# Encoder trunk: low parts, channel sums, first taps, reciprocals and sigmoids change engine or place

## The chip, the cores and the metric

The kernel runs on one core of a Trainium2 chip. The metric is the device time of one execution in microseconds (us). TensorE (PE) does the matmuls and the transposes, VectorE (DVE) and GpSimd (POOL) the elementwise work, ScalarE (ACT) the activations and scaled copies. Each engine works through its own queue in order, and waits there for semaphores of the others.

## The reference

Two sequences (256 and 512 tokens, 768 in all) go through two layers of the same shape; the width is 1024.

```python
def conv_module(u, w_dw, b_dw, ln_g, ln_b, w_pw):
    a, g = jnp.split(u, 2, axis=-1)
    z = a * jax.nn.sigmoid(g)
    z = lax.conv_general_dilated(z, w_dw[:, None, :], ...) + b_dw   # 31 taps, per channel
    z = jax.nn.silu(layer_norm(z, ln_g, ln_b))
    return z @ w_pw

for l in range(DEPTH):                       # 2 layers
    h = rms_norm(x, g_mix[l])
    q, k, v, u, gl = jnp.split(h @ w_in[l], splits, axis=-1)
    ...                                      # rms norm and rotary positions of q and k
    a = blocked_attention(q, k, v)           # 8 heads of 128, 2 heads of k and v
    c = conv_module(u, ...)
    ga, gc = jnp.split(jax.nn.sigmoid(gl + b_gate[l]), 2, axis=-1)
    x = x + (ga * a + gc * c) @ w_out[l]
    gate, up = jnp.split(rms_norm(x, g_ffn[l]) @ w_gu[l], 2, axis=-1)
    x = x + (jax.nn.silu(gate) * up) @ w_down[l]
return rms_norm(x, g_final)
```

## The kernel before

Matmuls are done in three passes over split operands: each float32 factor is a high part (rounded by ScalarE, names `hi_`) and a low part (the difference, names `lo_`), and hi·hi, lo·hi and hi·lo are summed. Of the weights ScalarE makes the high parts and GpSimd the low parts, in units of 128x1024 (two column tiles, `size == 2`) or in quarters; `wu` are the weights of the convolution's input u, `wqkv` those of q, k and v, `wgl` of the gates, `wpw` of the pointwise convolution, `wo` of the output projection, `wd` of the down projection.

A layer has these stretches. First come the projections for the convolution's input, k and q, then attention in 48 steps: a step is a head h and a tile t of 128 queries, named `h3t0` and so on. A step's scores (`h3t0s`) are three matmuls; VectorE takes the row maximum (TENSOR_REDUCE into `st`), ScalarE the exponential and its row sum, VectorE the reciprocal, ScalarE scales the probabilities (`h3t0p`), and TensorE transposes them (`h3t0T`) one step later. Between scores and transposes TensorE's queue has "fill": projections of v, q, u (`ug`, `ua`) and the gates (`gl`), later the pointwise convolution (`c`). After attention follow the output projection and the feed-forward part, the longest stretch.

The depthwise convolution is VectorE's. The 1024 channels are 8 tiles of 128; each tile's gated input is a padded buffer `z` (there are three, `N_Z = 3`), and its output `y` of 128x783 comes from 31 taps: the first is `y = z*w0 + b`, the others are `y = z*wk + y`. Sums of the eight `y` over the tiles go to `ysum`, the squares to `sq`. From them the channel norm is made: two matmuls with ones give `mean`, 8 centrings (`y - mean`, VectorE), 8 squares (ScalarE) and 7 adds (VectorE), six small matmuls `var`, an inverse root on GpSimd (`vs`), its spread `rb`, six transposes `rstd`, 8 scalings (VectorE), then silu and the split into `zsh` and `zsl`, which the pointwise convolution `c` multiplies.

The order is written out by the host program. `Clock` models TensorE's time as matmuls are issued (`now`) and VectorE's (`dve`, by 1/960 us per element and 0.13 per operation). Whenever the model shows VectorE less than 1.0 us ahead, it issues the next tap, from one of two tiles in turn; what is due at a time waits in a heap. Two places break this pace. A new `z` (in `ag_half`) is only begun when at most two are live, and until then all outstanding taps of the oldest are issued in one burst; GpSimd then zeroes the borders of the new `z` (the MEMSETs), which waits until the last tap on the old one is done. And before the first matmul of `c`, `pw_body` calls `force`, which issues, without any TensorE work between them, all taps and all parts of the channel norm that are still outstanding.

Of the kernel before, what the change touches and what calls it, by code (L numbers as in the profile page):

```python
# [13 lines left out]
F32 = mybir.dt.float32  # L14
F32R = mybir.dt.float32r
BF16 = mybir.dt.bfloat16
AF = mybir.ActivationFunctionType
ALU = mybir.AluOpType
AX = mybir.AxisListType

P = 128
D = 1024
KC = D // P
# [21 lines left out]
CONV_N = ZP - 2 * PAD  # L45

V_GMIX, V_GFFN, V_GFIN, V_BDW, V_LNG, V_LNB, V_BGATE, V_WDW = 0, 8, 16, 24, 32, 40, 48, 64
# [6 lines left out]
class Clock:  # L54
# [21 lines left out]
    def tick(self):  # L76
        while self.heap and self.heap[0][0] <= self.now:
            heapq.heappop(self.heap)[2]()
        while self.dve < self.now + TAP_AHEAD and self.tap():
            pass  # L80
# [38 lines left out]
class Vector:  # L119
# [5 lines left out]
    def __getattr__(self, name):  # L125
        f = getattr(self.engine, name)

        def call(out, *args, **kw):
            n = 1
            for d in (args[0].shape if name == "tensor_reduce" else out.shape)[1:]:  # L130
                n *= d
            self.clock.vector(n / 960.0 + 0.13)
            return f(out, *args, **kw)  # L133
        return call

# [20 lines left out]
def trunk(tc, x_in, x_tok, w_a, w_qkv, w_pw, w_out, w_gu, w_down, vecs, gqk, rope, y_out):  # L156
    nc = tc.nc
    clock = Clock()
    vector = Vector(nc.vector, clock)

    with ExitStack() as ctx:
        cst = ctx.enter_context(tc.tile_pool(name="cst", bufs=1))
# [35 lines left out]
        def vcol(l, base, j):  # L198
            return vec[:, l * VEC + base + j: l * VEC + base + j + 1]
# [88 lines left out]
        class Weights:  # L288
# [48 lines left out]
            def pump(self):  # L337
                while self.load():
                    pass
                if self.ready < len(self.all) and clock.now >= self.next:  # L340
                    w = self.all[self.ready]
                    if self.here(w) and self.live + w.size + max(self.staged, N_WS) <= N_W:
                        self.split()

            def get(self, w):
                while w.out is None:
                    self.split()
                return w.out

            def free(self, w):  # L350
# [278 lines left out]
        def layer_blocks(l):  # L629
            y = Layer()  # L630
# [126 lines left out]
            def conv(j, z):  # L757
                wcol = lambda k: vcol(l, V_WDW, k * KC + j)

                def first():  # L760
                    y.y[j] = UC(nm(f"y{j}"))
                    vector.tensor_scalar(y.y[j], z[:, :CONV_N], wcol(0), vcol(l, V_BDW, j), op0=ALU.mult, op1=ALU.add)

                def tap(k):
                    def f():
                        vector.scalar_tensor_tensor(y.y[j], z[:, k:k + CONV_N], wcol(k), y.y[j],
                                                    op0=ALU.mult, op1=ALU.add)
                    return f

                def last():  # L770
                    y.z_live -= 1
                    tap(CK - 1)()
                    clock.at(1.5, add)

                def add():
                    if y.ysum is None:
                        y.ysum = XP(nm("ysum"))[:, :CONV_N]
                        nc.gpsimd.tensor_copy(y.ysum, y.y[j])
                    else:
                        engine = vector if y.convs == KC - 1 else nc.gpsimd  # L780
                        engine.tensor_tensor(y.ysum, y.ysum, y.y[j], op=ALU.add)
                    y.convs += 1
                    if y.convs == KC:
                        clock.at(LN_AFTER, lambda: channel_norm(y))

                taps = [tap(k) for k in range(1, CK - 1)] + [last]
                clock.waiting.append([first] + taps)

            def ag_half(j, ws, w0, s, part):
                if s == 0:  # L790
# [63 lines left out]
            for b in FILL:  # L854
                kind, _, n = b.partition(":")
                n = int(n or 0)
# [258 lines left out]
            def down7(c0):  # L1115
# [40 lines left out]
                def then(b):  # L1156

                    after = list(BURSTS[b]) if b < len(BURSTS) else []
                    if tail and b == 3:
# [6 lines left out]
                def part(b):  # L1166
                    ms = BURSTS[b]

# [122 lines left out]
        def attention(y):  # L1291
            l, nm = y.l, y.nm
# [6 lines left out]
            def scores(n):  # L1299
                h, t, s, un = unit(n)  # L1300
                stream.until((l, f"q:{h // 2}"))
                for f in y.k_flip:
                    f()
                qs, fs = y.q[h // 2]
                fs[h % 2]()
                (qhi, qlo), (khi, klo) = qs[h % 2], y.k[h // GROUP]
                k0, nk = SPLITS[s]
                tk = slice(t * P, (t + 1) * P)
                sc = PS(un + "s")
                for p, (qq, kk) in enumerate(((qhi, khi), (qlo, khi), (qhi, klo))):  # L1310
                    mm(sc[:, :nk], qq[:, tk], kk[:, k0:k0 + nk], p == 0, p == 2)
                r = y.srq[h // 2][:, 2 * t + h % 2:2 * t + h % 2 + 1]
                sm = S(un + "st", 4)
                clock.tick()
                vector.tensor_reduce(sm[:, 0:1], sc[:, :nk], axis=AX.X, op=ALU.max, negate=True)
                p32 = HT(un + "p")
                probs[n] = p32

                def exp():
                    act(sm[:, 1:2], sm[:, 0:1], AF.Copy, scale=r)  # L1320
                    act(p32[:, :nk], sc[:, :nk], AF.Exp, scale=r, bias=sm[:, 1:2], accum_out=sm[:, 2:3])

                late = stream.done((l, FILL[-1]))
                jobs[n] = [
                    clock.later(A_EXP, exp),
                    clock.later(A_REC[late], lambda: vector.reciprocal(sm[:, 3:4], sm[:, 2:3])),
                    clock.later(A_SCALE[late], lambda: act(p32[:, :nk], p32[:, :nk], AF.Copy, scale=sm[:, 3:4])),
                ]

            def flip(n):  # L1330
                h, t, s, un = unit(n)
                nkt = SPLITS[s][1] // P
                if t % 2 == 0:
                    pairs[n // 2] = (XP(un + "pThi", (P, 4, 256), F32R), XP(un + "pTlo", (P, 4, 256), F32R))
                hi, lo = pairs[n // 2]
                p32 = probs.pop(n)
                for job in jobs.pop(n):
                    job()
                tp = PS(un + "T")
                for c in range(nkt):  # L1340
                    turn(tp[:, c * P:(c + 1) * P], p32[:, c * P:(c + 1) * P])
                t3 = tp[:, :nkt * P].rearrange("p (c q) -> p c q", q=P)
                dst = (slice(None), slice(0, nkt), slice((t % 2) * P, (t % 2 + 1) * P))
                clock.tick()
                act(hi[dst], t3)
                jobs.setdefault(("lo", n // 2), []).append(
                    clock.later(PT_LO, lambda: sub_lo(vector, lo[dst], t3, hi[dst])))
# [32 lines left out]
            def fill():  # L1380
                goal[0] += FILL_US / 2
                if not stream.done((l, FILL[-1])):
                    stream.run(goal[0], (l, FILL[-1]))
                    if stream.done((l, FILL[-1])):
                        goal[0] = stream.work
                        goal[0] += PW_START
                        y.late = clock.now + 8.0
                        y.h_free = 2
                        split_z(y)
                elif y.m_done:  # L1390
                    goal[0] = max(goal[0] + (LATE_US - FILL_US) / 2, stream.work)
                    stream.run(goal[0], (l, f"pw:{min(y.m_done, PW_MAX) - 1}"))

            NU = H * NT
            for n in range(NU + VLAG):
                if n < NU:
                    scores(n)
                if n >= VLAG and (n - VLAG) % 2 == 0:
                    values((n - VLAG) // 2)
                if n < NU and n % NT == 3 and n // NT % 2 == 0:  # L1400
                    y.q[n // NT // 2][1][1]()
                fill()
                if 1 <= n <= NU:
                    flip(n - 1)
                if clock.now >= y.late:
                    flush(y)
                fill()
            for f in outs:
                f()

# [3 lines left out]
        def channel_norm(y):  # L1414
# [59 lines left out]
            def scale(j):  # L1474
                def f():
                    for s, (t0, n) in enumerate(SPLITS):
                        sl = slice(YO[s], YO[s] + n)
                        vector.tensor_tensor(ys[j][:, sl], ys[j][:, sl], rstd[s][:, :n], op=ALU.mult)
                    if j in SILU_AT:
                        clock.at(0.5, lambda: silus(j))  # L1480
# [53 lines left out]
        nc.gpsimd.memset(ones, 1.0 / D)  # L1534
        nhalf = cst.tile([P, 16], F32, name="nhalf")
        nc.gpsimd.memset(nhalf, -0.5)


        y = layers[0]
# [69 lines left out]
        "gl:10", "gl:2", "q:2", "ag:7", "gl:3", "gl:14", "gl:12", "gl:4", "gl:11", "q:3", "gl:5", "gl:13", "gl:7",  # L1609
        "gl:15", "gl:6"]  # L1610
SILU_AT = (5, 7)
BURSTS = ((1, 7), (6, 4), (5, 2), (3,))
D_FIRST = (4.0, 6.0)
D_AT = 0.5
# [23 lines left out]
RSTD_AFTER = 5.4  # L1638
TABLES_AT = 16.0
TAP_AHEAD = 1.0  # L1640
W_STEP = (0.9, 2.9)
A_EXP = 2.2
A_REC = (4.5, 2.5)
A_SCALE = (4.9, 4.0)
PT_LO = 1.4
M_AT = 2.5
# [88 lines left out]
```

## Time and profile before

| | us |
|---|---|
| median of 3 runs (2399.19 to 2402.68) | 2401.75 |
| the profiled execution's own time | 2401.79 |
| its span, first to last instruction | 2400.0 |
| busy: TensorE, VectorE | 2235.7, 1933.2 |
| busy: ScalarE, GpSimd | 1134.3, 1285.0 |

The span lacks 1.8 us of the execution's own time, which lie before its first and after its last instruction. TensorE's granted clock is 0.972 of full speed over the whole span. Both layers show the same stretches at a distance of some 1187.5 us. Rows of a timeline join equal instructions that follow each other on an engine (x3); a bracket at the end gives the idle time before a row and who ended it.

### The profile page before, as it was taken

Reading aid. Unit: us, or ns where it says so; the run is one execution under the profiler, and the core shown is the slowest. Engines: PE = TensorE matmul, PEld = TensorE weight load, DVE = VectorE, ACT = ScalarE, POOL = GpSimd, SP = SyncE. Lnnn points to the kernel's source line nnn. Section 1 sums busy time; section 2 is a strip of 40 time slices with the busy share of each in tenths; the row PEclk is TensorE's granted clock in tenths of the full one; section 3 lists DMA queues with packets and bytes.
Section 4 is the critical chain, followed back from the end, with each engine's and each line's share of the span. In section 5 each row is a group of like instructions: output and inputs, shape, how many; then the busy total and the mean of one; then the engine's idle time right before and its main releaser. Section 6 shows DMA issues by size and latency. Waiting matters only on the chain. (4 is left out here: it accounts for less than half of the span.)

```text
span 2400.0 us, 34938 instructions
## 1 busy us (share of the span) xinstructions
PE 2235.7 (93%) x13276; PEld 2101.9 (88%) x13276; DVE 1933.2 (81%) x2480; ACT 1134.3 (47%) x2281; POOL 1285.0 (54%) x956
## 2 busy tenths in 40 slices
PE   8888898999979999999998899999999799999997
PEld 7878787888979999999987788878889799999997
DVE  5899999855387798798978999997553887887888
ACT  5425564684244444444443255647843444444443
POOL 4933554442266666666668344535323766756664
PEclk9999999999989999999999899999999899999999
DMA  4111111133313343343421111112341133334332
GB/s 168 36 62 62 52 58 60 64 101 137 113 44 110 119 141 123 124 141 110 156 82 53 53 47 57 58 62 78 111 170 53 44 121 135 129 118 141 123 123 88
DMA packets 72425, 229.60 MB, mean 96 GB/s; under 512 B 8128, under 2 KB 15296, under 8 KB 72256
## 3 DMA queue, kind: packets, MB, share of 16 engines
q1 hardware_dynamic: 72256, 227.37, 27.7%
q8 instruction: 104, 1.70, 0.3%
q14 instruction: 65, 0.53, 0.1%
HBM read 208.46 MB, written 18.87 MB: 95 GB/s over the span
## 5 line engine op out<-in xcount | busy, mean ns | idle before, releaser
L133 DVE SCALAR_TENSOR_TENSOR L_y<-L_z,vec,L_y 128x783 f32<-128x783 f32 x480 | 638.7, 1363 | 2.5
L214 POOL TENSOR_TENSOR wq_L_wgu_0m<-T_L_wgu,wq_L_wgu_0m 128x512 fp32r<-128x512 f32 x168 | 228.5, 1375 | 172.5 <-ACT wq_L_wgu_0m L211 172.5
L211 ACT ACTIVATE wq_L_wgu_0m<-T_L_wgu 128x512 fp32r<-128x512 f32 x168 | 102.7, 630 | 257.6 <-DVE T_L_wgu L133 204.4
L214 POOL TENSOR_TENSOR wq_L_wgu_0m<-st_L_wgu,wq_L_wgu_0m 128x512 fp32r<-128x512 f32 x126 | 179.3, 1424 | 43.3 <-ACT wq_L_wgu_0m L211 42.6
L203 PE MATMUL L_gl<-L_h1h,hi_L_wgl 128*128 128x512 f32 (+1 forms) x512 | 181.5, 355 | 0.3 <-DVE L_q3r L133 0.2
L203 PE MATMUL L_gl<-L_h1h,lo_L_wgl 128*128 128x512 f32 (+1 forms) x512 | 176.1, 344 | 0.0
L203 PE MATMUL L_gl<-L_h1l,hi_L_wgl 128*128 128x512 f32 (+1 forms) x512 | 176.0, 344 | 0.0
L214 POOL TENSOR_TENSOR lo_L_wgl<-st_L_wgl,hi_L_wgl 128x1024 fp32r<-128x1024 f32 x32 | 87.8, 2745 | 147.1 <-ACT hi_L_wgl L211 116.5
L214 POOL TENSOR_TENSOR lo_L_wqkv<-st_L_wqkv,hi_L_wqkv 128x1024 fp32r<-128x1024 f32 x24 | 69.0, 2877 | 137.1 <-ACT hi_L_wqkv L211 132.1
L214 POOL TENSOR_TENSOR lo_L_wu<-st_L_wu,hi_L_wu 128x1024 fp32r<-128x1024 f32 (+1 forms) x32 | 85.9, 2685 | 61.4 <-ACT hi_L_wu L211 61.4
L203 PEld LDWEIGHTS L_gl<-L_h1h,lo_L_wgl 128*128 128x128 f32 x512 | 99.0, 193 | 11.6
L203 PEld LDWEIGHTS L_gl<-L_h1h,hi_L_wgl 128*128 128x128 f32 x512 | 99.3, 194 | 10.7 <-DVE L_q3r L133 0.7
L203 PEld LDWEIGHTS L_gl<-L_h1l,hi_L_wgl 128*128 128x128 f32 x512 | 99.2, 194 | 10.3 <-issue 0.5
L214 POOL TENSOR_TENSOR lo_L_wo<-st_L_wo,hi_L_wo 128x1024 fp32r<-128x1024 f32 x16 | 39.6, 2476 | 116.0 <-ACT hi_L_wo L211 116.0
L203 PE MATMUL L_ua<-L_h1h,lo_L_wu 128*128 128x256 f32 (+1 forms) x256 | 89.0, 348 | 6.2 <-POOL lo_L_wu L214 6.1
L133 DVE TENSOR_TENSOR L_dl<-L_silu,L_dh 128x384 fp32r<-128x384 f32 x80 | 59.5, 782 | 41.0 <-ACT L_dh L211 41.0
L214 POOL TENSOR_TENSOR lo_L_wpw<-st_L_wpw,hi_L_wpw 128x1024 fp32r<-128x1024 f32 x16 | 40.0, 2502 | 97.0 <-ACT hi_L_wpw L211 92.2
L203 PE MATMUL L_ug<-L_h1h,lo_L_wu 128*128 128x256 f32 (+1 forms) x256 | 88.6, 346 | 2.3 <-DVE lo_L_wu L133 2.3
L203 PE MATMUL L_c<-L_zsh,hi_L_wpw 128*128 128x256 f32 (+1 forms) x256 | 90.4, 353 | 0.0
L203 PE MATMUL L_ug<-L_h1h,hi_L_wu 128*128 128x256 f32 (+1 forms) x256 | 89.8, 351 | 0.0
L203 PE MATMUL L_ua<-L_h1h,hi_L_wu 128*128 128x256 f32 (+1 forms) x256 | 89.8, 351 | 0.0
L211 ACT ACTIVATE wq_L_wgu_0m<-st_L_wgu 128x512 fp32r<-128x512 f32 x126 | 78.6, 623 | 22.9 <-POOL wq_L_wgu_0m L214 19.1
(1630 smaller groups left out, 7882.9 us busy)
## 6 DMA issues: line engine op xcount, KB each, us to landing
st_L_wgu<-w_gu SPq DMA_DIRECT2D x88, 512.0 KB, 3.5
st_L_wu<-w_a SPq DMA_DIRECT2D x32, 512.0 KB, 3.8
st_L_wgl<-w_a SPq DMA_DIRECT2D x32, 512.0 KB, 3.5
st_L_wqkv<-w_qkv SPq DMA_DIRECT2D x24, 512.0 KB, 3.6
st_L_wpw<-w_pw SPq DMA_DIRECT2D x16, 512.0 KB, 3.7
st_L_wo<-w_out SPq DMA_DIRECT2D x16, 512.0 KB, 3.7
g_dram<-L_sgl SPq DMA_DIRECT2D x16, 384.0 KB, 2.5
L_gj<-g_dram SPq DMA_DIRECT2D x16, 384.0 KB, 4.1
```

Of the source, the lines that this page charges most:

```text
L133: return f(out, *args, **kw)
L203: nc.tensor.matmul(out, lhsT, rhs, start=start, stop=stop)
L211: nc.scalar.activation(out, in_, func, **kw)
L214: engine.tensor_tensor(lo, x, hi.bitcast(F32), op=ALU.subtract)
```

## The change

Units of 128x1024 other than those of `wo` have their low parts made by VectorE (`engines`, called from `pump` and `get`); the `wo` units and the quarters stay on GpSimd. The sum `ysum` is begun by ScalarE (a copy) and added to by VectorE for all tiles, not only for the last. The first tap of a tile is a scaled copy with bias on ScalarE, issued 1.2 us (modelled) after the gate, and the other taps may follow 1.4 us after that. The reciprocal of the softmax sum becomes a power of -1 on GpSimd, 3.5 rather than 4.5 us after the scores. The sigmoids (`flush`) are issued after a step's second fill rather than before it. `TAP_MORE` has the value that stood in the formula before.

```diff
-            self.clock.vector(n / 960.0 + 0.13)
+            self.clock.vector(n / 960.0 + (TAP_MORE if n == CONV_N else 0.13))
...
-                        self.split()
+                        self.split(self.engines(w))
+            def engines(self, w):
+                return (vector if w.size == 2 and "_wo" not in w.name else nc.gpsimd,)
...
-                    vector.tensor_scalar(y.y[j], z[:, :CONV_N], wcol(0), vcol(l, V_BDW, j), op0=ALU.mult, op1=ALU.add)
+                    act(y.y[j], z[:, :CONV_N], AF.Identity, scale=wcol(0), bias=vcol(l, V_BDW, j))
...
-                        nc.gpsimd.tensor_copy(y.ysum, y.y[j])
+                        act(y.ysum, y.y[j])
                     else:
-                        engine = vector if y.convs == KC - 1 else nc.gpsimd
-                        engine.tensor_tensor(y.ysum, y.ysum, y.y[j], op=ALU.add)
+                        vector.tensor_tensor(y.ysum, y.ysum, y.y[j], op=ALU.add)
...
-                clock.waiting.append([first] + taps)
+                def ready():
+                    first()
+                    clock.at(FIRST_AT[1], lambda: clock.waiting.append(taps))
+                clock.at(FIRST_AT[0], ready)
...
-                    clock.later(A_REC[late], lambda: vector.reciprocal(sm[:, 3:4], sm[:, 2:3])),
+                    clock.later(A_REC[late], lambda: nc.gpsimd.tensor_tensor(sm[:, 3:4], sm[:, 2:3], nones, op=ALU.pow)),
...
                 fill()
                 if 1 <= n <= NU:
                     flip(n - 1)
+                fill()
                 if clock.now >= y.late:
                     flush(y)
-                fill()
...
+FIRST_AT = (1.2, 1.4)
+TAP_MORE = 0.13
...
-A_REC = (4.5, 2.5)
+A_REC = (3.5, 2.5)
```

Since the low parts and the sums count in the modelled time of VectorE, taps are issued later than before. Three places of the queues show what follows from that; both layers have the same order.

TensorE before, where `mean` stands, in the midst of step h4t5's gate matmuls:

```order
L203 MATMUL L_gl_0_4359<-L_h1h_183,hi_L_wgl_0_3958 128x256
L203 MATMUL L_gl_0_4359<-L_h1l_184,hi_L_wgl_0_3958 128x256
L203 MATMUL L_gl_0_4359<-L_h1h_183,lo_L_wgl_0_3959 128x256
L203 MATMUL L_mean_4377<-L_ysum,ones 128x256
L203 MATMUL L_mean_4379<-L_ysum,ones 128x512
L203 MATMUL L_gl_0_4359<-L_h1h_183,hi_L_wgl_0_3958 128x256
L203 MATMUL L_gl_0_4359<-L_h1l_184,hi_L_wgl_0_3958 128x256
```

TensorE after, between the last gate matmul of step h5t5 and the first matmuls of `c`:

```order
L203 MATMUL L_gl_1_4793<-L_h1h_352,lo_L_wgl_0_4439 128x512
L207 MATMUL L_h5t4T<-ident,L_h5t4p 128x128 x4
L203 MATMUL L_mean_4852<-L_ysum,ones 128x256
L203 MATMUL L_mean_4854<-L_ysum,ones 128x512
L203 MATMUL L_var<-ones,L_sq_4872 128x2 x6
L207 MATMUL L_rstd_4908<-ident,L_rb 128x128 x2
L207 MATMUL L_rstd_4911<-ident,L_rb 128x128 x4
L203 MATMUL L_c_0_4958<-L_zsh_4933,hi_L_wpw_0_4541 128x256
L203 MATMUL L_c_0_4958<-L_zsl_4934,hi_L_wpw_0_4541 128x256
```

Before, `mean`, `var` and `rstd` lie 154 and 53 rows apart, and `rstd` 83 rows ahead of `c`, with gate matmuls and attention steps between; after, all three have moved down into one piece directly ahead of `c`.

GpSimd after, around step h3t0 (`q2t`, `q2r` and `q2ss` belong to the rotary positions and the norm of the third pair of heads; rows with `nones` are the reciprocals):

```order
L1332 TENSOR_TENSOR L_h2t5st<-L_h2t5st,nones 128x1
L696 TENSOR_TENSOR L_q2t_3255<-L_q2t_3255,L_tab_447 128x4x32 x2
L698 TENSOR_TENSOR L_q2r_3026<-L_q2r_3026,L_q2t_3255 128x256
L803 MEMSET L_z_3343 128x15 x3
L696 TENSOR_TENSOR L_q2t_3316<-L_q2t_3316,L_tab_447 128x4x32 x2
L698 TENSOR_TENSOR L_q2r_3026<-L_q2r_3026,L_q2t_3316 128x256
L217 TENSOR_SCALAR L_q2ss<-L_q2ss 128x12
L218 TENSOR_TENSOR L_q2r<-L_q2ss,nhalf 128x12
L1332 TENSOR_TENSOR L_h3t0st<-L_h3t0st,nones 128x1
```

Step h3t0's reciprocal, which was in VectorE's queue before, now stands behind the MEMSETs of a new `z` and four more operations.

VectorE after, the last rows of the taps between the row maxima of h3t0 and h3t1 (18 taps, with one rotary product and two low parts; 1607 is the tile whose `z` the MEMSETs wait for):

```order
L133 SCALAR_TENSOR_TENSOR L_y_1607<-L_z_1438,vec,L_y_1607 128x783
L133 SCALAR_TENSOR_TENSOR L_y_2663<-L_z_2413,vec,L_y_2663 128x783
L133 SCALAR_TENSOR_TENSOR L_y_1607<-L_z_1438,vec,L_y_1607 128x783
L133 TENSOR_TENSOR L_h2t2m<-L_h2t2av,L_sgl_2924 128x256
L133 TENSOR_TENSOR L_ysum<-L_ysum,L_y_1607 128x783
L133 TENSOR_TENSOR lo_L_wgl_0_3390<-st_L_wgl_0_2869,hi_L_wgl_0_3389 128x1024
L133 TENSOR_TENSOR L_h2t4pTlo<-L_h2t5T,L_h2t4pThi 128x4x128
L133 TENSOR_REDUCE L_h3t1st<-L_h3t1s 128x1
```

Before, 7 taps stand between these two maxima, and neither a sum nor a low part; the burst has moved here.

## Rows read from the trace of the kernel before

**Rows 1.** Windows: length, each engine's busy us (instructions), granted clock, DMA share, GB/s.
```profile
53.00:516.00 463.00, 422.01 (x2703) 381.89 (x2702) 417.97 (x488) 240.55 (x531) 237.26 (x173) 0.96 0.18 59
170.00:185.00 15.00, 5.89 (x38) 5.52 (x37) 15.00 (x17) 5.28 (x9) 2.27 (x1) 0.78 0.01 1
178.00:188.50 10.50, 5.46 (x26) 5.46 (x27) 10.50 (x9) 5.28 (x9) 5.49 (x2) 0.51 0.16 51
515.00:680.00 165.00, 162.57 (x956) 151.89 (x956) 83.90 (x135) 74.64 (x136) 51.76 (x32) 0.99 0.33 115
```

**Rows 2.** Waits: engine, line, waited for; us in total, times, longest.
```profile
POOL L_z L797 <- DVE L_y L133: 30.0, 4, 11.3
...
PE L_h0t0T L207 <- ACT L_h0t0p L211: 19.8, 2, 10.7
...
PE L_h3t3T L207 <- ACT L_h3t3p L211: 11.1, 2, 5.5
```

**Rows 3.** Timeline 372 to 381: start us, us, engine, line, operation.
```profile
372.64 1.02 DVE L133 SCALAR_TENSOR_TENSOR L_y<-L_z,vec,L_y 128x783 f32<-128x783 f32 x1
...
374.92 5.07 DVE L133 SCALAR_TENSOR_TENSOR L_y<-L_z,vec,L_y 128x783 f32<-128x783 f32 x3
376.00 6.24 POOL L214 TENSOR_TENSOR lo_L_wgl<-st_L_wgl,hi_L_wgl 128x1024 fp32r<-128x1024 f32 x2 [8.81 <-ACT hi_L_wgl L211]
```

**Rows 4.** Groups by form: busy us, mean ns of one, idle before.
```profile
L133 DVE SCALAR_TENSOR_TENSOR L_y<-L_z,vec,L_y 128x783 f32<-128x783 f32 x480 | 638.7, 1363 | 2.5
...
L211 ACT ACTIVATE L_y<-L_y,vec 128x783 f32<-128x783 f32 x16 | 15.5, 1028 | 0.0
```

**Rows 5.** Tile view of wu's low parts: duration ns min/median/max.
```profile
L133 DVE TENSOR_TENSOR lo_L_wu<-st_L_wu,hi_L_wu x4: 672/1219/1758, 10.1 to 24.2; 128x512 fp32r<-128x512 f32 x4
```

**Rows 6.** Timeline of step h0t0: scores, row maximum, transposes.
```profile
161.99 0.28 PE L203 MATMUL L_h0t0s<-L_kTlo,L_q0Thi 128*128 128x256 f32 x1
...
178.66 0.41 DVE L133 TENSOR_REDUCE L_h0t0st<-L_h0t0s 128x1 f32<-128x256 f32 x1
...
183.04 0.69 PE L207 MATMUL L_h0t0T<-ident,L_h0t0p 128*128 128x128 f32 x2 [9.11 <-ACT L_h0t0p L211]
```

**Rows 7.** Timeline 357 to 365, GpSimd and VectorE.
```profile
357.19 2.21 POOL L692 TENSOR_TENSOR L_q2t<-L_q2t,L_tab 128x128 f32<-128x128 f32 x2
...
361.92 2.29 POOL L218 TENSOR_TENSOR L_q2r<-L_q2ss,nhalf 128x12 f32<-128x12 f32 x1
...
362.03 2.91 DVE L133 SCALAR_TENSOR_TENSOR L_y<-L_z,vec,L_y 128x783 f32<-128x783 f32 x3
```

**Rows 8.** Tile views of h3t0's scores and transposes, first start (and layer 2's).
```profile
L203 PE MATMUL L_h3t0s<-L_kTlo,L_q1Thi x2: 279/279/279, 341.8 to 1529.2; 128*128 128x256 f32 x2
...
L207 PE MATMUL L_h3t0T<-ident,L_h3t0p x4: 273/300/328, 355.5 to 1543.2; 128*128 128x128 f32 x4
```

**Rows 9.** Tile view of the mean; then the channel norm's timeline.
```profile
L203 PE MATMUL L_mean<-L_ysum,ones x8: 379/538/593, 452.3 to 1640.7; 128*128 128x256 f32 x4, 128*128 128x512 f32 x4
...
456.75 2.86 DVE L133 TENSOR_TENSOR L_y<-L_y,L_mean 128x256 f32<-128x256 f32 x6
...
474.08 1.98 DVE L133 TENSOR_TENSOR L_sq<-L_sq,L_sq 128x783 f32<-128x783 f32 x2 [0.39 <-ACT L_sq L211]
...
481.24 0.17 DVE L133 COPY L_vs<-L_var 128x6 f32<-128x6 f32 x1 [1.08 <-PE L_var L203]
...
482.75 1.32 POOL L218 TENSOR_TENSOR L_vs<-L_vs,nhalf 128x6 f32<-128x6 f32 x1
...
484.11 0.56 DVE L133 COPY L_rb<-L_vs 128x768 f32<-128x768 f32 x1 [0.31 <-POOL L_vs L218]
...
490.90 2.05 DVE L133 TENSOR_TENSOR L_y<-L_y,L_rstd 128x256 f32<-128x256 f32 x4 [2.36 <-PE L_rstd L207]
```

**Rows 10.** Timeline of ScalarE, 514 to 526.
```profile
514.54 1.28 ACT L211 ACT_TABLE_LOAD   x1
...
525.03 2.59 ACT L211 ACTIVATE L_sgl<-L_sgl,vec 128x768 f32<-128x768 f32 x3
```

## What the change should do to the time, predicted blind

> **What bounds the kernel now.** I read the windows first. From 515 us to 680 TensorE is busy 162.57 of 165 us at a clock of 0.99, so the output projection and the feed-forward part, where VectorE has half its time free, can give nothing [rows 1]. From 53 to 516 TensorE is busy 422.01 of 463 us, VectorE 417.97 [rows 1]. That stretch, and its copy in the second layer, is where the change works. It loses 41 us of idle TensorE per layer, and its granted clock of 0.96 means up to 0.04 x 463 = 18.5 us of lost speed, of which I take 16 beside the idle time. So 57 us per layer are to be had, no more.
>
> The waits name what ends them: TensorE waits 19.8 us in two places for h0t0's probabilities and 11.1 for h3t3's, GpSimd 30.0 for taps before it zeroes a new `z` [rows 2]. All lead to VectorE: h0t0's scores end at 162.3, its row maximum begins at 178.66, its transposes at 183.04 after 9.11 us of idle TensorE [rows 6], and around that VectorE is busy 15.00 of 15 us [rows 1]. After such a stall the clock is low: 178 to 188.5 ran at 0.51, TensorE resumed at 183.04, so 5.5 us at 1.2 GHz, which cost 2.7 [rows 1, 6].
>
> Why VectorE is late: a tap alone takes 1.02 us, but three taps from 374.92 took 5.07 while GpSimd made low parts for 6.24 us [rows 3]; the 480 taps average 1.363 [rows 4]. That is (1363 - 1020) x 240 = 82 us per layer of blocked taps. The Trainium skill states this as a rule ("SBUF — State Buffer", section "SBUF: two separate sides"): VectorE with two SBUF inputs and GpSimd hold one port pair in turn, for a whole instruction. The trace agrees for the low parts.
>
> **The change part by part, per layer.**
>
> Low parts to VectorE. A 128x512 one took 0.67 us at best [rows 5], so one of 1024 is some 1.2. A layer has 52 such units, some 46 of them ahead of 516: about 54 us. Against them stand the 82 us of blocked taps that go and 8 first taps that leave VectorE (5 us at best); six more sums come (6 us). VectorE thus gains some 27 us in all and should stay within TensorE's pace in most steps: of the old 57 us of loss I keep 2.
>
> What decides is that the low parts also count in the modelled VectorE time, so taps are issued later. I followed VectorE's queue from maximum to maximum with 0.95 us per tap and 1.13 per low part: most steps come to 5 to 9 us, three do not. Their costs:
>
> - h0t0. 69 taps and 14 low parts stand ahead of its maximum (80 taps before). I get the maximum 9 us behind the scores, and 6.2 us from there to the transposes (4.4 now [rows 6], plus the reciprocal's trip to GpSimd). TensorE has 183.04 - 9.11 - 162.3 = 11.6 us of fill. Stall 4 (0 to 9).
> - h1t5. A burst of 13 taps, 13 x 0.95 = 12.4 us, and low parts, 17.7 in all, stand ahead of its maximum, in a step of about 8.8 us: 8.9 us more behind the scores, 10.4 with a usual 1.5. With the 6.2 from there and some 12 us of fill, as at h0t0: stall 5 (2 to 6).
> - h3t0. Its reciprocal now stands on GpSimd behind the MEMSETs, which wait for the last of 18 taps after the maximum: 18 x 0.95 + 2 for what lies between = 19 us, and the maximum at least 1.5 us behind the scores. After them come two rotary products, the norm's power (2.29) and the reciprocal, about 5 us (357.19 to 364.2, 7.0, in the trace beside taps [rows 7]), and the scaling. Probabilities are ready 26.5 us after the scores; TensorE has 355.5 - 341.8 = 13.7 us of fill there, 12.5 without its own idle time [rows 8]. Stall 14 (10 to 18).
> - The channel norm. `mean` began at 452.3 and `c` after 510, with gate matmuls between [rows 9]; now nothing lies between, and TensorE waits through the chain. From mean: first centring at 1.7 us, eight of 0.93 (456.75: six halves, 2.86) to 9.1, the seven adds, 1.0 each (474.08: two, 1.98), to 16.1, `var` and its copy 1.4, the inverse root with its scale 1.7, `rb` 0.56, transposes 0.9, first scaling at 20.7, eight of 0.93 (490.90) to 28.1, `zsl` 0.43: `c` starts at 28.6, minus 3 us of TensorE's own small work [rows 9]. All scalings stand ahead of the first `zsl` on VectorE, so `c` can't begin on the first tile alone. Stall 26 (22 to 30).
> - h6t0 behind it. ScalarE first has eight silus of 1.03 [rows 4] with their splits, two table loads of 1.28 and three sigmoids of 0.86 [rows 10]. Stall 3 (0 to 5).
>
> Low clock behind these five stalls: 2.7 after long ones, 1 to 2 after short ones: 9 (6 to 12).
>
> First taps on ScalarE: 8 x 0.93 us on an engine busy 240 of 463 us [rows 1, 4]. Where the gate is late ScalarE waits with exponentials queued behind. I take 0 beyond the above, 4 at worst. Sigmoids after the second fill move table loads by a fill: 0, -2 to 2.
>
> Reciprocals on GpSimd. The skill's rule, read by the letter, would let each of 48 (about 0.55 us, as an estimate from the power of 12 elements) block a tap. The rows speak against it: three taps from 362.03 took 2.91 us, unblocked, while a power ran from 361.92 for 2.29 [rows 7]. By the rule 26 us more of VectorE per layer, some 5 of them in lagging steps, would give 2424; I go by the row, 0.
>
> Sum per layer: 2 + 4 + 5 + 14 + 26 + 3 + 9 = 63, against 57: +6. Two layers: +12 on 2401.8 of the profiled execution, which equals the median within 0.04: **2414**.
>
> **The rivals.**
>
> *A, faster.* The old stalls go and the new ones stay near their lower ends: h0t0 and h1t5 are caught up (2 together), h3t0 10, the chain 22 because centrings, squares and adds overlap better, clock 7, rest 2: 43, so -14 per layer, 2374; halfway 2385. For it: every old wait leads back to blocked taps [rows 2, 3], and this part is sure. Against it: the chain's order is fixed in three engines' queues.
>
> *B, no change to speak of* (within 0.2%, 4.8 us, about what a measurement of this kernel can tell): new stalls of 55 to 59 us per layer, a few less than I sum. Time 2402.
>
> *C, clearly slower: low parts late.* They now stand in VectorE's queue among bursts of taps, and gate matmuls wait for them. Where a low part of `wgl` stands behind the 18 taps at h3t0 or the 13 at h1t4, TensorE would stop ahead of the transposes. It decides from the point where a unit's lead, in fill, is shorter than the burst, about 12 to 17 us. Price: up to 6 more at each of the two bursts, 5 at h0t0 and 2 of clock, 19 per layer beyond mine less what coincides with the stalls named, say 13: 2440. For it: VectorE is in arrears at h0t0 already. Against it: in mid-stretch units are made several steps ahead.
>
> **How the numbers follow.** My forecast 0.43, C 0.15, A 0.27, B 0.15. So faster 0.27, same 0.15, slower 0.58. The bounds add to 40 to 84 per layer with all ends at once, 2368 to 2456; half of that to either side of the middle leaves 2 in 10 outside, drawn a little out for A and C: 2380 to 2443.
>
> **What would show it.** The change's trace should have: taps at a mean near 1.03 us; no long wait of h0t0T and none of h3t3T; one TensorE gap of some 14 us ahead of h3t0T, with GpSimd in the MEMSETs for `z`; and between `mean` and the first `c` some 29 us in which TensorE does 14 small matmuls. If `mean` to `c` is under 20 us, or `h3t0T` has no gap, the forecast is too slow and A holds. If taps stay near 1.3, contention has another source and the time is above my range. If TensorE waits for VectorE's low parts, C.

## The result and the profile after

The changed kernel takes 2443.97 us (2443.3 to 2444.4, four runs) against 2401.89 of the kernel before (four runs): ratio 1.0177, 95% interval 1.0164 to 1.019. The direction was forecast; the size, 42 us where 12 were forecast, was not, and the time lies just above the end of the range, 2443.

All of it arises ahead of the output projection. Its first matmul, by the tile view of `L_o` (duration min/median/max, first start, last), before and after:

```profile
L203 PE MATMUL L_o<-L_mThi,hi_L_wo x256: 331/337/427, 601.3 to 1857.1; 128*128 128x384 f32 x128
```
```profile
L203 PE MATMUL L_o<-L_mThi,hi_L_wo x256: 331/336/425, 622.0 to 1898.7; 128*128 128x384 f32 x128
```

601.3 has become 622.0: 20.7 us in the first layer. The last, in the second layer, is 41.6 us later. So a layer loses some 20 us, and what follows its attention gains or loses little.

The windows of the changed kernel (columns as in [rows 1]) show where:

```profile
290.00:350.00 60.00, 38.66 (x276) 36.10 (x276) 45.69 (x55) 25.49 (x63) 21.82 (x28) 0.83 0.10 34
452.00:540.00 88.00, 52.39 (x294) 45.79 (x293) 62.38 (x93) 54.56 (x89) 14.18 (x17) 0.77 0.15 51
490.00:524.00 34.00, 8.28 (x35) 7.50 (x36) 21.23 (x41) 16.49 (x22) 3.74 (x5) 0.50 0.00 0
622.00:690.00 68.00, 68.00 (x393) 67.78 (x392) 26.57 (x44) 20.41 (x35) 20.64 (x14) 1.00 0.25 91
```

Two stretches have a low clock and an idle TensorE: 290 to 350, where it is busy 38.66 of 60 us, and 452 to 540, with 52.39 of 88 at a clock of 0.77; inside it 490 to 524 ran at 0.50, 1.2 GHz. Behind them, from 622, nothing is lost. VectorE, 15.00 of 15 us busy in the stall of before [rows 1], is itself idle for 14 of the 60 and 26 of the 88 us: the kernel isn't short of VectorE there. The waits name the same places (us in total, times, longest):

```profile
POOL L_z L803 <- DVE L_y L133: 157.7, 10, 24.4
...
ACT L_h3t0p L211 <- POOL L_h3t0st L1332: 44.6, 2, 22.3
...
PE L_h3t0T L207 <- ACT L_h3t0p L211: 42.6, 2, 21.3
...
PE L_var L203 <- DVE L_sq L133: 40.3, 2, 20.1
...
PE L_h1t5T L207 <- ACT L_h1t5p L211: 13.0, 2, 6.5
PE L_h6t0T L207 <- ACT L_h6t0p L211: 9.9, 2, 5.7
PE L_c L203 <- DVE L_zsl L133: 9.5, 2, 4.7
```

h0t0T (0.5 us a layer now) and h3t3T of [rows 2] are gone from the head of the list; h3t0T, var, h1t5T, h6t0T and c have come, all named in the prediction. And the taps are freed, by the groups by form (busy us, mean ns of one), in place of 1363 ns in [rows 4]:

```profile
L133 DVE SCALAR_TENSOR_TENSOR L_y<-L_z,vec,L_y 128x783 f32<-128x783 f32 x480 | 496.1, 1077 | 0.8
...
L133 DVE TENSOR_TENSOR lo_L_wgl<-st_L_wgl,hi_L_wgl 128x1024 fp32r<-128x1024 f32 x32 | 40.5, 1266 | 44.6 <-ACT hi_L_wgl L211 44.6
```

The gap ahead of h3t0T, in the timeline of all engines (start us, us, engine, line, operation):

```profile
319.32 0.42 DVE L133 TENSOR_REDUCE L_h3t0st<-L_h3t0s 128x1 f32<-128x256 f32 x1
...
324.03 15.20 DVE L133 SCALAR_TENSOR_TENSOR L_y<-L_z,vec,L_y 128x783 f32<-128x783 f32 x16
...
339.29 0.20 POOL L803 MEMSET L_z<- 128x15 f32 x3 [19.29 <-DVE L_y L133]
...
342.33 2.29 POOL L218 TENSOR_TENSOR L_q2r<-L_q2ss,nhalf 128x12 f32<-128x12 f32 x1
344.59 0.54 POOL L1332 TENSOR_TENSOR L_h3t0st<-L_h3t0st,nones 128x1 f32<-128x1 f32 x1
...
345.72 0.69 PE L207 MATMUL L_h3t0T<-ident,L_h3t0p 128*128 128x128 f32 x2 [21.34 <-ACT L_h3t0p L211]
```

The row maximum starts at 319.32. Eighteen taps end at 339.2, then the MEMSETs run, then three operations of the rotary positions and two of q's norm, then the reciprocal at 344.59, and TensorE goes on after 21.3 us.

The channel norm, in the same view, rows of three engines in order of time:

```profile
484.43 1.56 PE L203 MATMUL L_mean<-L_ysum,ones 128*128 128x256 f32 x4 [0.18 <-DVE L_ysum L133]
...
487.16 7.51 DVE L133 TENSOR_TENSOR L_y<-L_y,L_mean 128x256 f32<-128x256 f32 x16
494.59 0.98 DVE L133 TENSOR_TENSOR L_sq<-L_sq,L_sq 128x783 f32<-128x783 f32 x1
...
495.60 0.85 ACT L211 ACTIVATE L_sq<-L_y 128x783 f32<-128x783 f32 x1 [4.67 <-DVE L_sq L133]
...
496.48 0.97 DVE L133 TENSOR_TENSOR L_sq<-L_sq,L_sq 128x783 f32<-128x783 f32 x1 [0.92 <-ACT L_sq L211]
...
506.10 2.72 PE L203 MATMUL L_var<-ones,L_sq 128*128 128x2 f32 x12 [20.11 <-DVE L_sq L133]
...
511.40 1.54 PE L207 MATMUL L_rstd<-ident,L_rb 128*128 128x128 f32 x6 [2.57 <-DVE L_rb L133]
...
515.24 0.58 PE L203 MATMUL L_c<-L_zsh,hi_L_wpw 128*128 128x256 f32 x1 [2.30 <-ACT L_zsh L211]
520.56 0.58 PE L203 MATMUL L_c<-L_zsl,hi_L_wpw 128*128 128x256 f32 x1 [4.74 <-DVE L_zsl L133]
520.94 0.41 PE L203 MATMUL L_c<-L_zsh,lo_L_wpw 128*128 128x256 f32 x1
```

From `mean` at 484.43 TensorE does next to nothing until the second matmul of `c` at 520.56. From the first add on, ScalarE's square waits for the add before it and the add for the square: 494.59 and 496.48 are 1.9 us apart.

### The profile page after: what moved, and what is told of

The parts are those of the page before. It is cut to its first block, busy times and chain, and to the rows that moved or that the text cites. A ratio compares the mean times of both kernels' runs of the same rounds, so it can differ in the third digit from the quotient of the medians.

```text
span 2441.5 us, 34896 instructions
## 1 busy us (share of the span) xinstructions
PE 2226.4 (91%) x13276; PEld 2095.6 (86%) x13276; DVE 1876.5 (77%) x2484; ACT 1143.8 (47%) x2289; POOL 1068.2 (44%) x935
## 5 line engine op out<-in xcount | busy, mean ns | idle before, releaser
L133 DVE SCALAR_TENSOR_TENSOR L_y<-L_z,vec,L_y 128x783 f32<-128x783 f32 x480 | 496.1, 1077 | 0.8
L203 PE MATMUL L_gl<-L_h1h,hi_L_wgl 128*128 128x512 f32 (+1 forms) x512 | 176.6, 345 | 0.0
L203 PE MATMUL L_c<-L_zsl,hi_L_wpw 128*128 128x256 f32 (+1 forms) x256 | 89.2, 348 | 9.5 <-DVE L_zsl L133 9.5
L203 PE MATMUL L_ug<-L_h1l,hi_L_wu 128*128 128x256 f32 (+1 forms) x256 | 89.5, 349 | 0.0
L203 PE MATMUL L_c<-L_zsh,lo_L_wpw 128*128 128x256 f32 (+1 forms) x256 | 88.9, 347 | 0.0
L203 PE MATMUL L_ua<-L_h1l,hi_L_wu 128*128 128x256 f32 (+1 forms) x256 | 88.1, 344 | 0.0
L203 PE MATMUL L_o<-L_mTlo,hi_L_wo 128*128 128x384 f32 x256 | 86.4, 338 | 0.0
```

The costliest lines, as they stand in the source:

```text
L203: nc.tensor.matmul(out, lhsT, rhs, start=start, stop=stop)
```

## The experiments

Two theories were set against each other. **Order**: the low parts are added to VectorE's modelled time; the host therefore issues taps later; so a new `z` has to force bursts, and the channel norm is left to `force`, bare ahead of `c`. **Amount**: VectorE has more work than it can do, and falls behind wherever the order puts it. All runs are of the two kernels with small edits. Each edited kernel was run once, but for one that was run four times. The kernel before, run beside them, had medians of 2399.9 to 2401.9 us, and seven of its runs lie between 2398.07 and 2404.55: a difference of 6 us or less between single runs says nothing here.

**Low parts not counted.**

```diff
-                return (vector if w.size == 2 and "_wo" not in w.name else nc.gpsimd,)
+                return (nc.vector if w.size == 2 and "_wo" not in w.name else nc.gpsimd,)
```

The same instructions run on the same engines; `nc.vector` only bypasses the model's counting.

> The changed kernel, with the low parts still on VectorE but not counted in its modelled time; so taps are issued as early as before and mean, var and rstd stand again among the gate matmuls. Theory 1 (order): the 44 us that TensorE loses between 452 and 601 in each layer go, unless GpSimd's reciprocals meet the MEMSETs elsewhere; about 2360 us (2335 to 2400). Theory 2 (too much work): VectorE, loaded with the same work earlier, falls behind step by step, and the stalls come back at the row maxima; 2420 to 2470.

Measured: 2358.16 us, 86 less than the changed kernel and 43 less than before. `mean` stands 341 rows ahead of `c` again and no burst is longer than 7 taps. VectorE does the same work, so amount falls as the cause of the loss. The 20 us ahead of `var` are gone:

```profile
PE L_var L203 <- DVE L_sq L133: 2.6, 2, 1.3
```

**The first part alone, counted and uncounted.** The kernel before with `engines` as in the diff above, in both forms, and nothing else changed.

> The kernel before with one part of the change alone: the low parts on VectorE, counted in its modelled time. Its order of TensorE's work has mean, var and rstd bare ahead of c, as in the changed kernel. Theory 1: taps at about 1.05 us, the stalls of before gone (-50 per layer), the bare norm there (+44 per layer), no h3t0 gap of 20 us since the reciprocals stay on VectorE: 2395 us (2380 to 2410). If the sums and first taps, which here stay where they were, are what unblocks the taps, then the mean tap stays over 1.15 us and the time is above 2420.

Measured: 2454.28 us, the mean tap 1096 ns. The taps are freed without the sums and the first taps, as expected, but the time is 59 us above the one expected: the gap ahead of h3t0T is there although the reciprocals are on VectorE, and `mean` itself waits.

```profile
PE L_var L203 <- DVE L_sq L133: 37.3, 2, 18.7
PE L_h3t0T L207 <- ACT L_h3t0p L211: 30.5, 2, 15.3
PE L_mean L203 <- DVE L_ysum L133: 22.3, 2, 11.3
```

So this part alone makes the whole loss, and more; the other parts give some 10 us of it back.

> The kernel before with the low parts on VectorE, not counted in its modelled time: the order of taps is exactly that of before. Theory 1: taps near 1.09 us as in the counted run, mean among the gate matmuls, stalls of before mostly gone: 2376 us (2360 to 2395). Theory 2 (VectorE overloaded): above 2400.

Measured: 2397.11 us, the mean tap 1119 ns. Counting alone is worth 57 us here, 86 on the changed kernel. But it is only 3 us below the kernel before, less than single runs can tell from nothing, and just outside the range I gave. In attention its stalls are small and many (none over 4 us), and most row maxima between h0t4 and h4t4 start 5 to 11 us behind their scores. So in this order VectorE does run behind; but it does so by much the same in the kernel before (4 to 10 us in these steps) and in the uncounted kernel (4 to 11), so this lag isn't what sets the three apart. The other parts of the change are worth 39 us on top (2397 against 2358); which of them it is, beside the reciprocals' 15 below, wasn't separated.

**Taps counted for less.** `TAP_MORE` is the fixed part of a tap in the model; low parts stay counted.

```diff
-TAP_MORE = 0.13
+TAP_MORE = 0.0      # and 0.05 in a second kernel
```

> The changed kernel with TAP_MORE 0 in place of 0.13: low parts stay counted, but a tap counts 0.82 us, so taps are issued earlier and in no burst over 7; mean and rstd stand among gate matmuls again (245 and 43 rows ahead of c). Theory 1 (order): 2370 us (2355 to 2395), no gap over 6 us. Theory 2 (too much work): 2420 or more.

Measured: 2379.08 us, in the range of the first theory: 65 less than the changed kernel with the same work for VectorE. No wait of TensorE in attention is over 5.4 us.

> The changed kernel with TAP_MORE 0.05: between the changed kernel (0.13, 2444 us) and 0 (2379 us). No burst over 8 taps; mean is 132 rows ahead of c, but var and rstd are still bare ahead of it. If bursts and the bare norm cost as the gaps show: the h3t0 gap of 21 us is gone, of the norm's 31 us from mean to c about 12 stay with what follows: 2395 us (2380 to 2410). If the work on VectorE counts and not its order, it stays above 2425.

Measured: 2369.87 us, below the range I gave, and 9 below `TAP_MORE` 0 where I had expected it above; why 0.05 is the better of the two stays open. `var`, `rstd` and `c` stand one behind another in it as in the changed kernel; only `mean` is 132 rows earlier, and no burst is over 8 taps. TensorE idles 0.8 us or less ahead of `var` rather than 20; the waits at `rstd`, `c` and h6t0T, 15 us in a layer, are still there. So the loss that this run takes back is that of the cover from `mean` to `var`, and that of the h3t0 gap, which is now 4.0 us.

```profile
PE L_h3t0T L207 <- ACT L_h3t0p L211: 8.0, 2, 4.0
...
PE L_var L203 <- DVE L_sq L133: 1.5, 2, 0.8
```

From 0.13 to 0.05 is 74 us for one number in the model, with the same instructions on every engine.

**The reciprocals back on VectorE**, on the changed kernel and on the uncounted one.

```diff
-nc.gpsimd.tensor_tensor(sm[:, 3:4], sm[:, 2:3], nones, op=ALU.pow)
+vector.reciprocal(sm[:, 3:4], sm[:, 2:3])
...
-A_REC = (3.5, 2.5)
+A_REC = (4.5, 2.5)
```

> The changed kernel with the softmax reciprocals back on VectorE, 4.5 us after the scores. Theory 1 (order): the 21.3 us gap ahead of h3t0T comes from the reciprocal that stands on GpSimd behind the MEMSETs; it goes, and with it the half clock behind it, some 20 us per layer; mean still stands directly ahead of var and c, so the 31 us there stay. About 2403 us (2396 to 2412). Theory 2 (VectorE simply has too much work and is in arrears at h3t0): the gap stays or only moves behind the 18 taps to h3t1; 2430 to 2445.

Measured: 2461.95 us, 18 more, where both theories had it no slower than the changed kernel. The timeline shows why the gap stays:

```profile
328.34 18.03 DVE L133 SCALAR_TENSOR_TENSOR L_y<-L_z,vec,L_y 128x783 f32<-128x783 f32 x19
...
347.51 0.15 DVE L133 RECIPROCAL L_h3t0st<-L_h3t0st 128x1 f32<-128x1 f32 x1
```

On VectorE the reciprocal stands behind 19 taps of the same burst. My reading that without its move to GpSimd's queue there is no gap was wrong; the burst makes one in either queue. And as the reciprocals count in the model too, taps come later still: `mean` now waits 10.2 us for `ysum`.

> Both edits: reciprocals on VectorE and low parts not counted. Theory 1: neither the h3t0 gap nor the bare channel norm; what is left is the gain from unblocked taps, up to 57 us per layer less a few: 2320 us (2300 to 2350). Theory 2: VectorE in arrears, 2400 or more.

Measured: 2373.45 us, 15 more than with the reciprocals on GpSimd; above the range of the first theory, below that of the second. Unblocked taps and neither of the two gaps thus don't bring the 57 us per layer: many small waits stay. The move is a gain of 15 to 18 us as long as GpSimd has no low parts to make; a part of it can be the order, since reciprocals on VectorE count and taps then come later. With low parts on GpSimd, on the kernel before:

> The kernel before with the reciprocals on GpSimd alone. GpSimd still makes the low parts, 2.4 to 3.1 us each, and a reciprocal can stand behind one or two. If that is why the run with low parts back on GpSimd was 15 us slower than before: 2412 us (2405 to 2425), with gaps ahead of transposes that wait for GpSimd. If GpSimd has room, it is a gain of up to 10 us as on the changed kernel: 2385 to 2400.

(The same diff on the kernel before, with A_REC as in the change and a tile of minus ones.) Measured: 2432.27 us, 30 more than before, above the range. By its waits and timeline a reciprocal now stands behind a low part, the MEMSETs and q's norm:

```profile
359.78 2.81 POOL L214 TENSOR_TENSOR lo_L_wgl<-st_L_wgl,hi_L_wgl 128x1024 fp32r<-128x1024 f32 x1 [2.80 <-ACT hi_L_wgl L211]
...
368.93 0.54 POOL L1326 TENSOR_TENSOR L_h3t0st<-L_h3t0st,nones 128x1 f32<-128x1 f32 x1
...
ACT L_h3t0p L211 <- POOL L_h3t0st L1326: 19.6, 2, 9.8
```

The reciprocals, no longer counted on VectorE, also bring taps forward (`mean` 52 rows earlier), so more taps stand ahead of the row maxima; how the 30 us are shared between the two wasn't measured.

**The MEMSETs on VectorE**, behind the taps they wait for.

```diff
-                        nc.gpsimd.memset(part["z"][:, o:o + PAD], 0.0)
+                        nc.vector.memset(part["z"][:, o:o + PAD], 0.0)
```

> The changed kernel with the zeroing of a new z's borders on VectorE, behind the taps that it waits for anyway; GpSimd's queue is free for the reciprocals. If the burst of 18 taps is the root, the gap ahead of h3t0T goes, but h3t1's row maximum still stands behind the burst, some 22 us behind its scores, and a gap of 8 to 14 us opens ahead of h3t1T: in all 2425 us (2412 to 2440). If the MEMSETs in GpSimd's queue are the root, both gaps stay away: 2400 us (2390 to 2410).

Measured: 2420.16 us, 24 less. The 21 us ahead of h3t0T become 4.8, and another 4.8 appears ahead of h3t2s:

```profile
PE L_h3t2s L203 <- DVE L_h2t2m L133: 9.6, 2, 4.8
PE L_h3t0T L207 <- ACT L_h3t0p L211: 9.6, 2, 4.8
```

The first is q's norm on GpSimd, behind which the reciprocal still stands:

```profile
323.19 2.95 POOL L218 TENSOR_TENSOR L_q2r<-L_q2ss,nhalf 128x12 f32<-128x12 f32 x1
326.11 1.11 POOL L1332 TENSOR_TENSOR L_h3t0st<-L_h3t0st,nones 128x1 f32<-128x1 f32 x1
```

The second is the burst's, on another tile than I had named: a product behind the 18 taps. So with the reciprocals on GpSimd the burst costs some 5 us by itself, and some 16 of the 21 by way of the MEMSETs in GpSimd's queue. On the uncounted kernel the same edit:

> The two edits that gained, together: low parts on VectorE but not counted, and the borders of a new z zeroed on VectorE. The uncounted run alone had 2358 us and still a gap of 4.1 us ahead of h3t0T, where the reciprocal stands behind the MEMSETs. If that wait is what is left there: 2350 us (2340 to 2358). If VectorE's own arrears are: 2358 to 2365.

Measured: 2360.29 us (2358.02 to 2361.26, four runs), ratio to before 0.9825, 95% interval 0.9808 to 0.9841; no better than the uncounted kernel's 2358.16. The 4 us ahead of h3t0T are there as before. In the uncounted kernel's timeline the MEMSETs aren't what the reciprocal waits for; the reciprocal stands behind q's norm:

```profile
325.37 0.20 POOL L803 MEMSET L_z<- 128x15 f32 x3
...
330.00 2.29 POOL L218 TENSOR_TENSOR L_q2r<-L_q2ss,nhalf 128x12 f32<-128x12 f32 x1
332.25 1.16 POOL L1332 TENSOR_TENSOR L_h3t0st<-L_h3t0st,nones 128x1 f32<-128x1 f32 x1
```

Where no burst of 18 taps stands ahead of them, moving the MEMSETs gained nothing. Both versions beat the kernel before and the changed one.

**Low parts back on GpSimd**, all else as changed: the diff of the first experiment with `return (nc.gpsimd,)`.

> The changed kernel with the low parts back on GpSimd: first taps, sums, reciprocals and sigmoids as changed. Its order of taps is that of the run with uncounted low parts, tap for tap, so the two differ by the engine of the low parts alone. Theory 1 (blocked taps are what VectorE gains): taps at 1.25 to 1.35 us beside GpSimd's low parts, and the time 25 to 50 us above 2358: 2395 us (2380 to 2410). If the order alone made that run fast, this one is at 2360 or less, since VectorE has 60 us per layer less to do.

Measured: 2415.10 us, above the range, the mean tap 1334 ns. Its taps are issued in the order of the uncounted run, tap for tap; moving the low parts to VectorE is worth 57 us there, in spite of VectorE's 60 us of added work per layer. That is the gain the change was after. Not all of it need be freed taps: with low parts on GpSimd the reciprocals there stand behind them, and ScalarE waits 130 us for reciprocals over both layers, 67 in the uncounted run. How the 57 us are shared wasn't separated. With the reciprocals and the sums where the kernel before has them, the same move in an unchanged order was worth 3 us, as shown above.

```profile
L133 DVE SCALAR_TENSOR_TENSOR L_y<-L_z,vec,L_y 128x783 f32<-128x783 f32 x480 | 621.5, 1334 | 4.7 <-ACT L_y L211 2.3
...
ACT L_h3t0p L211 <- POOL L_h3t0st L1332: 19.6, 2, 9.8
```

**More buffers for the squares.**

```diff
-                    sq = Z(nm(f"sq{j}"))
+                    sq = (UC if j > 2 else Z)(nm(f"sq{j}"))
```

> The changed kernel with the squares of tiles 3 to 7 in buffers of another set, so that ScalarE's next square needn't wait until VectorE has added the one before. If the ping-pong of square and add (1.9 us per tile, where I had counted 1.0) is what made the channel norm longer than I summed, var comes 4 to 6 us earlier in each layer: 2433 us (2429 to 2438). If VectorE's queue sets the pace there, 2444.

Measured: 2434.52 us, in the range, 9.5 less, 4.7 per layer. The wait ahead of `var` falls from 20.1 to 16.1 us:

```profile
PE L_var L203 <- DVE L_sq L133: 32.1, 2, 16.1
```

So the ping-pong of squares and adds through three buffers is a part of the norm's length that I hadn't seen.

## Why the prediction was right or wrong

**The bound and what there was to gain: right for this kernel.** Next to nothing is gained or lost behind 601 or 622; of the 57 us per layer, stalls and low clock of before, all but some 2 went, as I had kept. (In the uncounted kernel, whose layer is some 22 us shorter than before, small waits take up the rest.) Taps came to 1077 ns, where I had written 1030: rotary products on GpSimd still slow some (last section).

**The mechanism was right in its main steps; the sum was too small: 63 us of new loss per layer, where some 77 came** (57 of before and the 20.7 by which `L_o` starts later). What the terms measured, by TensorE's gaps and the clock behind them:

| per layer, us | forecast, with its clock | measured |
|---|---|---|
| channel norm and h6t0 | 33 | 44 |
| h3t0 | 17 | 23 |
| h1t5 | 6 | 8 |
| h0t0 | 5 | 0 |
| kept | 2 | 2 |
| sum | 63 | 77 |

The forecast column shares the 9 us of low clock as the prediction's prices per stall have it. The measured column is time in which TensorE did less than its usual pace, in stretches of 50 to 100 us, and holds the clock; it is good to a us or so. By matmuls priced at their usual distance from start to start (0.118 us for 256 columns, 0.23 for 512), 240 to 290 lose 8.8 us, 290 to 350 23.1 and 452 to 540 43.1. What was kept is the rest of the 77, not a reading of its own.

**The step that failed: the channel norm, mis-sized by 11 us with h6t0 behind it.** I had `c` running 28.6 us behind `mean`; its second matmul, the first that needs `zsl`, comes 36.1 us behind. The adds took 11.5 us from 494.59 to 506.1, not 7: I had priced the seven adds back to back from two rows of before that stood together, and [rows 9] could have told me that an add waits for its square there. `sq_u` confirms this with 4.7 us. `var` and its copy took 2.9, not 1.4, since the matmuls of `var` ran at the low clock (2.72 us), and a low part and a probability split stood ahead of the first centring (487.16, 2.7 us behind `mean` rather than 1.7). The eight scalings took 8.0 us, not 7.4: the row that I read, 2.05 us for four halves, gives 8.2. These four make up the 7.5 us. Of the low clock I had counted 2.7 us after a long stall; here the whole stretch from 490 to 524 ran low, `c` began at 1.2 GHz (0.41 us for a matmul of 128x256 at 520.94, where one at full clock takes 0.28 [rows 6]), and after the wait of 5.7 us at h6t0T, for which I had 3, it ran low again (0.70 from 535 to 545).

**h3t0 was mis-sized, by 6 us.** The terms hold one by one: 20.0 us from the maximum to the MEMSETs (forecast 19), 6.4 from there to the transposes (some 6), 12.1 us of fill (12.5). But I let the maximum begin 1.5 us behind the scores; it began 7.0 behind (scores end at 312.3): VectorE still had taps and rotary products in its queue, and waited 1.5 us for ScalarE between them. The path by way of the MEMSETs is the one I named, and moving them took 16 of the 21 us away. What I didn't see is that the burst is the root: with the reciprocal back on VectorE (`rec_dve`) there is a gap of 17.2 us in the same place. At h1t5 the maximum was 12.4 us late rather than 10.4, for a gap of 6.5 rather than 5.

**h0t0 was wrong the other way.** The maximum came 6.1 us behind the scores, not 9: VectorE ran less far behind than I had followed it. Its stall of 4 didn't come (0.5).

**Rivals.** (A's halfway mark should read 2388, not 2385: half of 14 us in each of two layers.) A would have been right in its mechanism had the norm been hidden: the uncounted kernel, with the same instructions, is at 2358 us, below A's 2374. So A's case against, that the chain's order is fixed in three queues, carried it. B fell. C's time, 2440, was closest, but its mechanism wasn't there: no wait of TensorE for low parts of `wgl` stands in the list; low parts waited for ScalarE's high parts instead (44.6 us in all, at VectorE). The longest of these waits, 6.2 us, stands behind the burst at h3t0, where TensorE is running again; but 0.8 us stand ahead of its 16 taps and so in the stall. What they cost in all wasn't measured.

**What the row on the power was worth.** I went by [rows 7] against the letter of the Trainium skill's rule, and took 0 for the reciprocals beside taps. That holds, as the last section shows, and the reciprocals on GpSimd turned out a gain of 15 to 18 us, order included, where I had expected none.

## What to carry to other kernels

When work moves to an engine whose modelled time paces the order, ask first what the planner will then issue later, and what it must then issue in one piece: here the same instructions on the same engines differ by 86 us for being counted. Price a chain that loses its cover link by link with the rows of each link's waits, not with rows that happen to stand back to back, and count the low clock for the small matmuls inside a long stall as well as for those behind it. And when an operation waits in a queue, look for what it would wait for in the other queue before taking the move for the cause. A burst of taps costs in both.

## What the runs showed of the hardware

A reciprocal of one element per partition on GpSimd didn't slow a tap, a rotary product did. Of the taps of the changed kernel, the 278 beside which GpSimd did nothing took 1028 ns on average, the 72 beside a reciprocal alone 1029, the 108 beside rotary products alone 1220. The price is paid on the other side: the reciprocal took 0.54 us where no tap, product or sum of VectorE was running as it began (35 times), and 1.07 on average, up to 1.38, where a tap was (48 times); on VectorE it takes 0.15. In the changed kernel, VectorE and GpSimd:

```profile
96.29 3.90 DVE L133 SCALAR_TENSOR_TENSOR L_y<-L_z,vec,L_y 128x783 f32<-128x783 f32 x3
...
96.85 1.35 POOL L698 TENSOR_TENSOR L_q0r<-L_q0r,L_q0t 128x256 f32<-128x256 f32 x1
...
467.65 2.92 DVE L133 SCALAR_TENSOR_TENSOR L_y<-L_z,vec,L_y 128x783 f32<-128x783 f32 x3
...
469.04 0.98 POOL L1332 TENSOR_TENSOR L_h5t3st<-L_h5t3st,nones 128x1 f32<-128x1 f32 x1 [6.75 <-ACT L_h5t3p L211]
...
477.04 0.54 POOL L1332 TENSOR_TENSOR L_h5t4st<-L_h5t4st,nones 128x1 f32<-128x1 f32 x1 [7.03 <-ACT L_h5t4p L211]
477.11 3.17 DVE L133 SCALAR_TENSOR_TENSOR L_y<-L_z,vec,L_y 128x783 f32<-128x783 f32 x3
```

Three taps took 3.90 us beside rotary products, 2.92 with a reciprocal begun in their midst (which took 0.98) and 3.17 with one begun just before them (which took 0.54); beside low parts, as [rows 3] has it, 5.07. The Trainium skill ("SBUF — State Buffer", section "SBUF: two separate sides") lets whichever of the two begins first, a VectorE operation with two SBUF inputs or a GpSimd operation that reads SBUF, hold the shared pair for its whole instruction, while the other waits. The trace agrees for wide operations of GpSimd, and for most reciprocals that begin behind a tap; it shows no such cost for the 32 taps that begin while nothing but a reciprocal is running (1030 ns on average).
